# Sums of weight blocks made by accumulating DMAs instead of VectorE and GpSimd, in a float32 hybrid convolution block

## The chip, the cores and the metric

The kernel runs on one core of one Trainium2 chip. A core has TensorE (PE; its weight load is listed apart as PEld), VectorE (DVE), ScalarE (ACT), GpSimd (POOL) and SyncE (SP, which only issues DMAs), and 16 DMA engines that all queues share. The metric is the device time of one execution in microseconds; a comparison uses the median of several runs.

## What is computed

One block on a sequence of 1024 positions with 1024 channels, all in float32. Cut to what matters here:

```python
h = rms_norm(x, norm_mix_g) * (1.0 + sc1) + sh1
b_s, c_s, v_s, v_c, gl_c, gate_br = split(h @ w_in)          # 7 x 1024 columns
y_a = (b_s * causal_dwconv(c_s * v_s, conv_short_w)) @ w_short_out
u = causal_dwconv(v_c * sigmoid(gl_c), conv_conf_w) + conv_conf_b
y_b = silu(layer_norm(u, conf_ln_g, conf_ln_b)) @ w_conf_out
g_a, g_b = split(sigmoid(gate_br))
x = x + g1 * ((g_a * y_a + g_b * y_b) @ w_o)
h2 = rms_norm(x, norm_ffn_g) * (1.0 + sc2) + sh2
a, b = split(h2 @ w_ffn_in)
x = x + g2 * ((silu(a) * b) @ w_ffn_out)
return rms_norm(x, final_norm_g)
```

## The kernel before

**Products.** Two tricks shape the work. First, a float32 product is made of three passes of TensorE: an operand is split into a rounded part (`wh`, a copy on ACT, line 234) and a remainder (`wl`, a subtraction, line 235, on DVE or POOL), and likewise the activations (`th`, `tl`); then wh by th, wh by tl and wl by th are added up in PSUM (`mm3`, lines 397, 398 and 400). Second, the large products are done by Strassen's scheme in Winograd's form: a pair of output row blocks, called a *dual*, has four weight blocks of 128 x 1024 ("11", "12", "21", "22"), and seven products stand in place of eight. They run in the order `PRODUCTS = "1265734"`. Product 1 uses block 11 and product 2 block 12. Product 6 uses s2 = 11 + (21 + 22), product 5 uses s1 = 21 + 22, product 7 uses 21 + 11, product 3 uses 12 + s2 and product 4 block 22. So each dual needs four sums of weight blocks. One product is 24 matmuls of 128 x 512.

**Stages.** A lead part makes the first products of h. Then come 13 duals of the input projection (`w_duals`, the last six matrices of `w_in` and the rest of the gates; 87 products, 88 to 562 us), two duals of the short convolution's projection (`w_short`, "ya", to 643 us), the projections `w_conf` and `w_o`, and the feed-forward part, which has duals of its own (`dual_units` with DVE, `last_units`) that the change doesn't touch. Beside the 13 duals DVE computes the long convolution (`conv`, line 972) and POOL adds up its result (`tot`, line 993). In the ya stage DVE also makes the layer norm's squares (lines 1015 and 1021) and multiplies with the gates, which POOL loads from DRAM (`ga`, line 1088).

**Units.** The weights of a product are made by a *unit*: it loads blocks (SP, line 218) into `raw` tiles, makes the sums that it needs, and splits the result (`split_w`). `next_w` calls `fetch`, which keeps three units begun: the one in use and two ahead. There are five `raw` tiles in turn (three of `rawp`, two of `rawbp`), and three `wh` and three `wl` tiles. So the rounding of a unit waits until TensorE has left the `wh` of the unit three before it.

**Who sums and splits.** The 13 duals are in three groups. Dual 0 has everything on DVE. Of dual 1 the units 1, 2 and 5, and of dual 2 the units 1 and 2, are on DVE, the rest on POOL. Duals 3 to 12 are wholly on POOL, sums and remainders. Both ya duals are on DVE. Duals 0 to 2 and the ya duals use `apart_units`, which loads blocks shortly before use, some of them twice; duals 3 to 12 use `dual_units`, which loads the four blocks once, with unit 1, and sums in lines 254, 257, 259 and 301. The sums of `apart_units` are line 312.

**Order.** A planner puts each engine's instructions in an order when the kernel is built, by its own estimate of when each is ready, with the order of the program as priority; `tc.issue_after(x)` holds an instruction behind x on the same engine. On the chip each engine then takes its instructions strictly in that order, and waits where one isn't ready. A DMA that needs data of another one waits on the queue of the engine that issues it.

Of the kernel before, what the change touches and what calls it, by code (L numbers as in the profile page):

```python
# [38 lines left out]
ALU = mybir.AluOpType  # L39
# [28 lines left out]
BEGUN = 2  # L68
# [47 lines left out]
PRODUCTS = "1265734"  # L116
# [15 lines left out]
def block_kernel(ctx: ExitStack, tc: tile.TileContext, x0, xT, c, vecs, ada, w_first, w_plain, w_duals,  # L132
                 w_short, w_conf, w_o, w_fi, w_fo0, w_fo1, outT):
    nc = tc.nc
# [42 lines left out]
    def f32(t):  # L177
        return t.bitcast(F32)
# [30 lines left out]
    def raw_tile(n=1024, home=None):  # L209

        if home is None:
            raws.append(raws.pop(0))
        return (home or raws[-1]).tile([P, 1024], F32, tag="raw", name="raw")[:, :n]

    def load(src, n=1024, home=None):
        raw = raw_tile(n, home)
        with tc.issue_after(x1_load[0]) if x1_load else ExitStack():
            load.ins = nc.sync.dma_start(raw, src).ins
        return raw
# [8 lines left out]
    def split_w(raw, n, after=(), lo_engine=nc.vector):  # L228
        wh = whp.tile([P, 1024], F32R, tag="wh", name="wh")[:, :n]
        wl = wlp.tile([P, 1024], F32R, tag="wl", name="wl")[:, :n]  # L230
        with ExitStack() as order:
            for ins in after:
                order.enter_context(tc.issue_after(ins))
            hi = nc.scalar.copy(wh, raw)  # L234
            lo = lo_engine.tensor_tensor(wl, raw, f32(wh), ALU.subtract)  # L235
        split_w.hi, split_w.lo = hi.ins, lo.ins
        if n == T and lo_engine is nc.gpsimd:
            pool_los.append((hi.ins, lo.ins))
        return wh, wl

    def dual_units(mats, n, early=0, eng=nc.vector):


        a = {}

        def get(*blocks):
            for b in blocks:
                a[b] = load(mats[("11", "12", "21", "22").index(b)], n)

        def sums(which, after=None):  # L250

            if "1" in which:
                a["s1"] = a["22"] if early == 2 else raw_tile(n)
                eng.tensor_tensor(a["s1"], a["21"], a["22"], ALU.add)
            with tc.issue_after(after) if after else ExitStack():
                if "3" in which:
                    eng.tensor_tensor(a["21"], a["21"], a["11"], ALU.add)
                if "2" in which:
                    dual_units.ins = eng.tensor_tensor(a["11"], a["11"], a["s1"], ALU.add).ins

        def begin():

            with tc.issue_after(load.ins):
                get("21", "22")
            yield
            eng.tensor_tensor(a["22"], a["21"], a["22"], ALU.add)
            with tc.issue_after(load.ins):
                get("11")
            yield
            a["s2"] = s2p.tile([P, T], F32, tag="x1", name="s2")[:, :n]  # L270
            with tc.issue_after(mix.half_0):
                eng.tensor_tensor(a["s2"], a["11"], a["22"], ALU.add)
            yield

        def unit_begun(m):
            get(*{"1": ("11",), "2": ("12",), "5": ("21", "22"), "7": ("11", "12"), "4": ("22",)}.get(m, ()))
            if m == "5":
                sums("1")
            elif m == "7":
                sums("3")  # L280
                eng.tensor_tensor(a["12"], a["12"], a["s2"], ALU.add)
            return split_w(a[{"1": "11", "2": "12", "6": "s2", "5": "s1", "7": "21", "3": "12", "4": "22"}[m]], n, (), eng)

        def unit(m, after=None):
            if "s2" in a:
                return unit_begun(m)
            if early == 2:
                get(*{"1": ("11",), "2": ("12",), "6": ("21", "22", "11"), "3": ("12",), "4": ("22",)}.get(m, ()))
            elif early:
                get(*{"1": ("11",), "2": ("12", "21", "22", "11")}.get(m, ()))  # L290
            elif m == "1":
                get("11", "12", "21", "22")
            if m in "12":
                w = split_w(a["1" + m], n, (), eng)
                if eng is nc.gpsimd:
                    sums("13" if m == "1" else "2")
                return w
            if m == "6" and eng is not nc.gpsimd:
                sums("132", after)
            if m == "3":  # L300
                eng.tensor_tensor(a["12"], a["12"], a["11"], ALU.add)
            return split_w(a[{"6": "11", "5": "s1", "7": "21", "3": "12", "4": "22"}[m]], n, (), eng)

        return {m: (lambda *after, m=m: unit(m, *after)) for m in PRODUCTS} | {"begin": begin()}

    def apart_units(mats, eng, on_eng=PRODUCTS, after=None):


        a = {}

        def add(out, x, y):
            unit.eng.tensor_tensor(out, x, y, ALU.add)  # L312
            return out

        def get(b):
            return load(mats[("11", "12", "21", "22").index(b)])

        def unit(m):
            unit.eng = eng if m in on_eng else nc.gpsimd
            if m in "12":  # L320
                raw = get("1" + m)
            elif m == "6":
                for b in ("21", "22", "11"):
                    a[b] = get(b)
                with tc.issue_after(after()) if after else ExitStack():
                    a["s1"] = add(a["22"], a["21"], a["22"])
                    if "6" in on_eng:
                        raw = a["s2"] = add(raw_tile(), a["11"], a["s1"])
                    else:
                        a["s3"] = add(a["21"], a["21"], a["11"])  # L330
                        raw = a["s2"] = add(a["11"], a["11"], a["s1"])
            elif m == "7":
                raw = a["s3"] if "s3" in a else add(a["21"], a["21"], a["11"])
            elif m == "3":
                raw = get("12")
                add(raw, raw, a["s2"])
            else:
                raw = a["s1"] if m == "5" else get("22")
            return split_w(raw, 1024, (), unit.eng)

        return {m: (lambda m=m: unit(m)) for m in PRODUCTS}

    plan = [None] * KC
    plan += [(w_plain[0], 1024)]
    n_duals = len(PAIRS) // 2
    win_units = [apart_units([w_duals[d, m] for m in range(4)], nc.vector, PRODUCTS if d == 0 else "125" if d == 1 else "12",
                             (lambda: t_split.ins) if d == 1 else None) for d in range(BEGUN + 1)]
    win_units += [dual_units([w_duals[d, m] for m in range(4)], 1024, eng=nc.gpsimd) for d in range(BEGUN + 1, n_duals)]
    win_order = [(BEGUN, m) for m in "12"] + [(d, m) for d in range(BEGUN + 1) for m in PRODUCTS[2:]]
    win_order += [(d, m) for d in range(BEGUN + 1, n_duals) for m in PRODUCTS]  # L350
    plan += [win_units[d][m] for d, m in win_order]
    ya_order = [(d, m) for m in "12" for d in range(2)] + [(d, m) for d in range(2) for m in PRODUCTS[2:]]
    ya_units = [apart_units([w_short[d, m] for m in range(4)], nc.vector) for d in range(2)]
    plan += [ya_units[d][m] for d, m in ya_order]
    plan += [(w[k], 1024) for w in (w_conf, w_o) for ks in (range(KC), SECOND[KEPT:]) for k in ks]
    ready = []
# [186 lines left out]
    x = {}  # L543
# [351 lines left out]
    b = {}  # L895
# [794 lines left out]
```

## Time and profile before

| What | us |
|---|---|
| median of 3 runs (1460.18 to 1462.07) | 1462.01 |
| the profiled execution | 1462.66 |
| its span, first to last instruction | 1460.9 |
| busy: PE, DVE, ACT, POOL | 1448.1, 1188.5, 627.2, 516.3 |

The profile is a page about one execution, and a trace that can be asked for more: groups of instructions, waits, the DMA issues with their time to landing, and timelines. A row of a timeline has the start, the duration, the engine, the line of the kernel, the operation, what it writes and reads, and how often it stands there in a row; in brackets, how long the engine was idle before it and what ended that. A row on one tile has the smallest, the median and the largest duration in ns, and the first and last start in us. Matmuls are pipelined and their ends are modelled, so their starts tell more than their durations.

### The profile page before, as it was taken

Reading aid. Unit: us, or ns where it says so; the run is one execution under the profiler, and the core shown is the slowest. Engines: PE = TensorE matmul, PEld = TensorE weight load, DVE = VectorE, ACT = ScalarE, POOL = GpSimd, SP = SyncE. Lnnn points to the kernel's source line nnn. Section 1 sums busy time; section 2 is a strip of 40 time slices with the busy share of each in tenths; the row PEclk is TensorE's granted clock in tenths of the full one; section 3 lists DMA queues with packets and bytes.
Section 4 is the critical chain, followed back from the end, with each engine's and each line's share of the span. In section 5 each row is a group of like instructions: output and inputs, shape, how many; then the busy total and the mean of one; then the engine's idle time right before and its main releaser. Section 6 shows DMA issues by size and latency. Waiting matters only on the chain.

```text
span 1460.9 us, 17711 instructions
## 1 busy us (share of the span) xinstructions
PE 1448.1 (99%) x6394; PEld 1187.8 (81%) x6394; DVE 1188.5 (81%) x1634; ACT 627.2 (43%) x911; POOL 516.3 (35%) x484
## 2 busy tenths in 40 slices
PE   9999999999999999999999999999999999999997
PEld 4878888888888888788888888888888888888887
DVE  7897999987988979999787698777777666866676
ACT  4773333333333346465235465444444443322235
POOL 0007777677677761111021001111111005662505
PEclk9999999999999999999999999999999999999999
DMA  9542222323222357476685436655554449996903
GB/s 351 206 139 85 73 94 79 116 73 101 72 87 73 123 201 281 130 233 206 209 293 203 152 101 216 214 178 198 169 177 148 143 148 327 395 392 193 359 1 116
DMA packets 88522, 257.68 MB, mean 176 GB/s; under 512 B 10177, under 2 KB 12865, under 8 KB 88434
## 3 DMA queue, kind: packets, MB, share of 16 engines
q1 hardware_dynamic: 43792, 142.04, 29.1%
q0 software_dynamic: 40608, 101.92, 21.2%
q10 hardware_dynamic: 4034, 12.59, 2.4%
q8 instruction: 50, 0.82, 0.2%
q14 instruction: 38, 0.31, 0.1%
HBM read 190.97 MB, written 65.54 MB: 176 GB/s over the span
## 4 chain that ended last, share of the span: by engine, by line
PE 88%; issue 4%; DVE 3%; POOL 2%; DMA 1%; ACT 1%; POOLq 0%; DVEq 0%; ACTq 0%
PE bank L400 11%; PE bank L397 11%; PE bank L398 11%; PE x L400 8%; PE x L398 8%; PE x L397 8%; PE z L397 3%; PE z L398 3%; PE z L400 3%; PE mix L400 2%; PE mix L397 2%; PE yb L400 2%; PE yb L397 2%; PE mix L398 2%; PE yb L398 2%
## 5 line engine op out<-in xcount | busy, mean ns | idle before, releaser
L234 ACT CAST wh<-raw 128x1024 fp32r<-128x1024 f32 (+3 forms) x255 | 260.9, 1026 | 475.5 <-PE bank L398 149.5
L235 DVE TENSOR_TENSOR wl<-raw,wh 128x1024 fp32r<-128x1024 f32 (+3 forms) x176 | 209.1, 1190 | 49.3 <-ACT wh L234 46.6
L235 POOL TENSOR_TENSOR wl<-raw,wh 128x1024 fp32r<-128x1024 f32 x79 | 191.4, 2426 | 105.4 <-ACT wh L234 105.3
L972 DVE SCALAR_TENSOR_TENSOR c<-diff,vec,c 128x512 f32<-128x512 f32 x232 | 168.4, 752 | 2.7
L1331 POOL DMA_DIRECT2D hid<-stage x70 | 37.3, 533 | 343.9 <-DVE stage L438 332.5
L400 PE MATMUL bank<-th,wl 128*128 128x512 f32 x312 | 121.5, 389 | 0.4 <-POOL wl L235 0.4
L398 PE MATMUL bank<-tl,wh 128*128 128x512 f32 x312 | 121.4, 389 | 0.0
L397 PE MATMUL bank<-th,wh 128*128 128x512 f32 x312 | 121.4, 389 | 0.0
L972 DVE SCALAR_TENSOR_TENSOR c<-u,wsum,c 128x512 f32<-128x512 f32 x112 | 84.4, 753 | 2.3
L400 PEld LDWEIGHTS bank<-th,wl 128*128 128x128 f32 x312 | 58.6, 188 | 13.0 <-POOL wl L235 0.8
L398 PEld LDWEIGHTS bank<-tl,wh 128*128 128x128 f32 x312 | 58.6, 188 | 12.2
L398 PE MATMUL x<-tl,wh 128*128 128x512 f32 x176 | 68.5, 389 | 0.0
L397 PE MATMUL x<-th,wh 128*128 128x512 f32 x176 | 68.5, 389 | 0.0
L400 PE MATMUL x<-th,wl 128*128 128x512 f32 x176 | 68.4, 390 | 0.0
L397 PEld LDWEIGHTS bank<-th,wh 128*128 128x128 f32 x312 | 58.6, 188 | 12.1
L437 ACT CAST stage<-g 128x512 fp32r<-128x512 f32 x60 | 37.3, 621 | 68.0 <-DMA hid<-stage 42.9
L438 DVE TENSOR_TENSOR stage<-g,stage 128x512 fp32r<-128x512 f32 x60 | 41.3, 690 | 27.2 <-ACT stage L437 27.1
L1355 POOL DMA_DIRECT2D th<-hid x77 | 41.2, 535 | 53.5 <-PE x L400 23.4
L312 POOL TENSOR_TENSOR raw<-raw 128x1024 f32<-128x1024 f32 x8 | 20.5, 2567 | 110.0 <-ACT th L437 104.9
L400 PE MATMUL yb<-zsh,wl 128*128 128x512 f32 x128 | 49.8, 389 | 0.0
L397 PE MATMUL yb<-zsh,wh 128*128 128x512 f32 x128 | 49.8, 389 | 0.0
L398 PE MATMUL yb<-zsl,wh 128*128 128x512 f32 x128 | 49.8, 389 | 0.0
(829 smaller groups left out, 4135.4 us busy)
## 6 DMA issues: line engine op xcount, KB each, us to landing
hid<-stage POOLq DMA_DIRECT2D x70, 512.0 KB, 4.7
raw<-in_w_duals SPq DMA_DIRECT2D x57, 512.0 KB, 3.5
raw<-in_w_fi SPq DMA_DIRECT2D x54, 512.0 KB, 4.7
th<-hid POOLq DMA_DIRECT2D x77, 256.0 KB, 6.0
tl<-hid POOLq DMA_DIRECT2D x77, 256.0 KB, 6.1
ada<-in_ada SPq DMA_DIRECT2D x24, 512.0 KB, 5.7
raw<-in_ada SPq DMA_DIRECT2D x24, 512.0 KB, 4.9
raw<-in_w_fo SPq DMA_DIRECT2D x16, 512.0 KB, 6.1
```

The source lines that it names most:

```text
L234: hi = nc.scalar.copy(wh, raw)
L235: lo = lo_engine.tensor_tensor(wl, raw, f32(wh), ALU.subtract)
L312: unit.eng.tensor_tensor(out, x, y, ALU.add)
L397: nc.tensor.matmul(ps, wh, xh, start=first, stop=False, skip_group_check=again)
L398: nc.tensor.matmul(ps, wh, xl, start=False, stop=False, skip_group_check=again)
L400: mm3.ins = nc.tensor.matmul(ps, wl, xh, start=False, stop=last, skip_group_check=again).ins
L437: t_split.act = nc.scalar.copy(hi, src).ins
L438: t_split.ins = nc.vector.tensor_tensor(lo, src, f32(hi), ALU.subtract).ins
L972: tap.ins = nc.vector.scalar_tensor_tensor(out=out, in0=src[:, s : s + H], scalar=wt, in1=acc, op0=ALU.mult, op1=ALU.add).ins
L1331: nc.gpsimd.dma_start(hid_dram[key], s)
L1355: nc.gpsimd.dma_start(t, hid_dram[key][:, s])
```

## The change

`apart_units` is replaced by `sum_units`, which serves all 13 input duals and both ya duals. Each sum is an accumulating DMA that POOL issues: the first block is loaded by SP as before, and the DMA adds the second block, from DRAM, onto it in the `raw` tile. For s2 the second operand is s1, from its own `raw` tile. So s2 waits for two loads and one accumulation, and s1 stays as it is for unit 5. Product 3's weights are made in the tile of s2. Which engine makes the remainder of which unit stays the same (`on_vector`).

```diff
-    def apart_units(mats, eng, on_eng=PRODUCTS, after=None):
+    def sum_units(mats, on_vector=PRODUCTS):
...
             if m in "12":
-                raw = get("1" + m)
+                raw = load(mat["1" + m])
             elif m == "6":
-                for b in ("21", "22", "11"):
-                    a[b] = get(b)
-                with tc.issue_after(after()) if after else ExitStack():
-                    a["s1"] = add(a["22"], a["21"], a["22"])
-                    if "6" in on_eng:
-                        raw = a["s2"] = add(raw_tile(), a["11"], a["s1"])
-                    else:
-                        a["s3"] = add(a["21"], a["21"], a["11"])
-                        raw = a["s2"] = add(a["11"], a["11"], a["s1"])
+                a["s1"] = load(mat["22"])
+                nc.gpsimd.dma_start(a["s1"], mat["21"], accum_op=ALU.add)
+                raw = a["s2"] = load(mat["11"])
+                nc.gpsimd.dma_start(raw, a["s1"], accum_op=ALU.add)
             elif m == "7":
-                raw = a["s3"] if "s3" in a else add(a["21"], a["21"], a["11"])
+                raw = load(mat["21"])
+                nc.gpsimd.dma_start(raw, mat["11"], accum_op=ALU.add)
             elif m == "3":
-                raw = get("12")
-                add(raw, raw, a["s2"])
+                raw = a["s2"]
+                nc.gpsimd.dma_start(raw, mat["12"], accum_op=ALU.add)
             else:
-                raw = a["s1"] if m == "5" else get("22")
-            return split_w(raw, 1024, (), unit.eng)
+                raw = a["s1"] if m == "5" else load(mat["22"])
+            return split_w(raw, 1024, (), nc.vector if m in on_vector else nc.gpsimd)
...
-    win_units = [apart_units([w_duals[d, m] for m in range(4)], nc.vector, PRODUCTS if d == 0 else "125" if d == 1 else "12",
-                             (lambda: t_split.ins) if d == 1 else None) for d in range(BEGUN + 1)]
-    win_units += [dual_units([w_duals[d, m] for m in range(4)], 1024, eng=nc.gpsimd) for d in range(BEGUN + 1, n_duals)]
+    win_units = [sum_units([w_duals[d, m] for m in range(4)], (PRODUCTS, "125", "12", "")[min(d, BEGUN + 1)])
+                 for d in range(n_duals)]
...
-    ya_units = [apart_units([w_short[d, m] for m in range(4)], nc.vector) for d in range(2)]
+    ya_units = [sum_units([w_short[d, m] for m in range(4)]) for d in range(2)]
```

More of the change, by code (lines that the diff above doesn't have):

```diff
@@ L304, in dual_units @@
         return {m: (lambda *after, m=m: unit(m, *after)) for m in PRODUCTS} | {"begin": begin()}
-    def apart_units(mats, eng, on_eng=PRODUCTS, after=None):
+    def sum_units(mats, on_vector=PRODUCTS):
         a = {}
[L311 to L316, printed above, removed]
+        mat = dict(zip(("11", "12", "21", "22"), mats))
         def unit(m):
-            unit.eng = eng if m in on_eng else nc.gpsimd
             if m in "12":
-                raw = get("1" + m)
+                raw = load(mat["1" + m])
             elif m == "6":
-                for b in ("21", "22", "11"):
-                    a[b] = get(b)
-                with tc.issue_after(after()) if after else ExitStack():
-                    a["s1"] = add(a["22"], a["21"], a["22"])
-                    if "6" in on_eng:
-                        raw = a["s2"] = add(raw_tile(), a["11"], a["s1"])
-                    else:
-                        a["s3"] = add(a["21"], a["21"], a["11"])
-                        raw = a["s2"] = add(a["11"], a["11"], a["s1"])
+                a["s1"] = load(mat["22"])
+                nc.gpsimd.dma_start(a["s1"], mat["21"], accum_op=ALU.add)
+                raw = a["s2"] = load(mat["11"])
+                nc.gpsimd.dma_start(raw, a["s1"], accum_op=ALU.add)
             elif m == "7":
-                raw = a["s3"] if "s3" in a else add(a["21"], a["21"], a["11"])
+                raw = load(mat["21"])
+                nc.gpsimd.dma_start(raw, mat["11"], accum_op=ALU.add)
             elif m == "3":
-                raw = get("12")
-                add(raw, raw, a["s2"])
-            else:
-                raw = a["s1"] if m == "5" else get("22")
-            return split_w(raw, 1024, (), unit.eng)
+                raw = a["s2"]
+                nc.gpsimd.dma_start(raw, mat["12"], accum_op=ALU.add)
+            else:
+                raw = a["s1"] if m == "5" else load(mat["22"])
+            return split_w(raw, 1024, (), nc.vector if m in on_vector else nc.gpsimd)
         return {m: (lambda m=m: unit(m)) for m in PRODUCTS}
```

## The prediction

> **What bounds the kernel now.** I read the page's first part, then PE's waits (who waited for whom: us in total, times, longest), then busy time by stretch (the stretch, its length, then PE, PEld, DVE, ACT and POOL with their counts, clock, DMA share, GB/s), and last the timelines of the two places where PE waits.
>
> ```profile
> PE 1448.1 (99%) x6394; PEld 1187.8 (81%) x6394; DVE 1188.5 (81%) x1634; ACT 627.2 (43%) x911; POOL 516.3 (35%) x484
> ...
> PE bank L400 <- DVE wl L235: 0.5, 1, 0.5
> PE bank L400 <- POOL wl L235: 0.4, 1, 0.4
> PE lead L398 <- DVE h41l L488: 0.3, 1, 0.3
> PE z L397 <- DVE g L1296: 0.2, 1, 0.2
> ...
> 156.00:535.00 379.00, 379.00 (x1674) 313.83 (x1673) 337.14 (x487) 135.03 (x184) 282.10 (x124) 1.00 0.27 89
> 535.00:645.00 110.00, 109.45 (x474) 88.61 (x473) 103.65 (x135) 62.90 (x96) 22.09 (x25) 1.00 0.68 230
> ```
>
> PE is busy for 99% of the span. A modelled end can hide a gap, so I look at the starts as well.
>
> ```profile
> 246.66 0.39 PE L397 MATMUL bank<-h41h,wh 128*128 128x512 f32 x1
> ...
> 252.10 0.39 PE L397 MATMUL bank<-th,wh 128*128 128x512 f32 x1
> ...
> 257.54 0.39 PE L397 MATMUL bank<-h00h,wh 128*128 128x512 f32 x1
> ...
> 268.42 0.39 PE L397 MATMUL bank<-t2h,wh 128*128 128x512 f32 x1
> ...
> 148.24 0.39 PE L398 MATMUL bank<-tl,wh 128*128 128x512 f32 x1
> 149.05 0.50 PE L400 MATMUL bank<-th,wl 128*128 128x512 f32 x1 [0.42 <-POOL wl L235]
> ...
> 612.68 0.39 PE L400 MATMUL bank<-q4h,wl 128*128 128x512 f32 x1
> 613.09 0.50 PE L397 MATMUL bank<-q6h,wh 128*128 128x512 f32 x1
> 613.43 0.39 PE L398 MATMUL bank<-q6l,wh 128*128 128x512 f32 x1
> 614.35 0.50 PE L400 MATMUL bank<-q6h,wl 128*128 128x512 f32 x1 [0.53 <-DVE wl L235]
> 614.69 0.40 PE L397 MATMUL bank<-q6h,wh 128*128 128x512 f32 x1
> ```
>
> The first four rows are the first matmuls of the products 3 and 4 of one dual and of 1 and 6 of the next. From 246.66 to 252.10 are 5.44 us for 24 matmuls, 0.227 us each, and 257.54 to 268.42 is twice that: PE runs at its own pace. From 156 to 535 us it never waits. Only two waits of PE lie where the changed sums are made. At 148 us a matmul starts 0.81 us after the one before it, 0.58 over the pace, and the one behind it 0.11 late: 0.7 us, for a remainder on POOL. At 613 us the four steps of 0.41, 0.34, 0.92 and 0.34 are 1.1 us over four times 0.227, for a remainder on DVE. Together 1.8 us: that is all that the change can give here, 0.12% of the time. (A measurement of this kernel tells about 0.2%, 2.9 us, from no change.)
>
> **What is removed.**
>
> ```profile
> L312 DVE TENSOR_TENSOR raw<-raw x12: 1220/1224/1240, 77.8 to 623.7; 128x1024 f32<-128x1024 f32 x12
> ...
> L312 POOL TENSOR_TENSOR raw<-raw x8: 2395/2400/3269, 107.8 to 144.2; 128x1024 f32<-128x1024 f32 x8
> ...
> L254 POOL TENSOR_TENSOR raw<-raw x10: 2402/2407/2412, 169.4 to 511.4; 128x1024 f32<-128x1024 f32 x10
> ...
> 144.24 2.40 POOL L312 TENSOR_TENSOR raw<-raw 128x1024 f32<-128x1024 f32 x1 [1.30 <-DMA raw<-in_w_duals]
> 146.59 7.12 POOL L235 TENSOR_TENSOR wl<-raw,wh 128x1024 fp32r<-128x1024 f32 x3
> ...
> 597.71 1.22 DVE L312 TENSOR_TENSOR raw<-raw 128x1024 f32<-128x1024 f32 x1
> ...
> 608.33 1.23 DVE L312 TENSOR_TENSOR raw<-raw 128x1024 f32<-128x1024 f32 x1
> ...
> 610.67 1.23 DVE L312 TENSOR_TENSOR raw<-raw 128x1024 f32<-128x1024 f32 x1
> ...
> 613.07 1.23 DVE L235 TENSOR_TENSOR wl<-raw,wh 128x1024 fp32r<-128x1024 f32 x1
> ```
>
> Sixty sums, four for each of 15 duals. DVE loses 12 of 1.22 us, 14.7 us, of which 8 lie in the short projection's stage. POOL loses 8 of 2.4 us (L312) and four for each of the ten duals that it sums itself (L254 and its like L257, L259, L301): 48 in all, 115 us. Neither engine bounds anything from 156 to 535 us, where POOL is busy 282 of 379 us and PE never waits, so there the gain is nothing. It is 0.7 us at 148 us, where POOL held the late remainder (146.59) behind a sum that had stood for a DMA (144.24). It is 1.1 us at 613 us, where DVE ran without a pause and took two sums (608.33, 610.67) right ahead of the remainder that PE waited for (613.07): without them that one is 2.4 us earlier, with the sum at 597.71 gone too 3.7, more than it was late.
>
> **What is added: 60 accumulating DMAs of 512 KB, issued by POOL, and 15 loads more on SP.** An input dual that POOL summed takes four loads now, and six loads and four accumulations afterwards. From 156 to 535 us the DMA engines are busy 0.27, so two and a half times as many transfers stay under 0.7; from 535 to 645 us the share is 0.68, and there 14 loads become 12 with 8 accumulations on top, which press on it for a while. Such an accumulation isn't in this trace. The nearest rows:
>
> ```profile
> raw<-in_w_duals SPq DMA_DIRECT2D x57, 512.0 KB, 3.5
> ...
> hid<-stage POOLq DMA_DIRECT2D x70, 512.0 KB, 4.7
> ...
> x<-x_dram POOLq DMA_DIRECT2D x8, 512.0 KB, 5.6
> ...
> cv<-cv SPq DMA_DIRECT2D x8, 512.0 KB, 7.0
> ...
> ga<-gate_a POOLq DMA_DIRECT2D x16, 256.0 KB, 4.1
> ...
> L1331 POOL DMA_DIRECT2D hid<-stage x70 | 37.3, 533 | 343.9 <-DVE stage L438 332.5 <-ACT stage L437 7.8 <-issue 2.9
> ```
>
> Issuing costs POOL 0.53 us, 32 us for sixty, against the 115 us taken off. The landing time L lies between 3.5 us (a load by SP of the same size) and 11.2 us (twice the 5.6 us of a DRAM-to-SBUF load by POOL, since the destination is read as well); I take 5.6, the same direction, size and queue. What L costs depends on what waits for it. POOL has to wait for the first accumulation of unit 6 (21 onto 22) before it issues the second (that sum onto 11), and behind it wait its next remainders. In the steady part, one dual to the next:
>
> ```profile
> 237.31 2.40 POOL L235 TENSOR_TENSOR wl<-raw,wh 128x1024 fp32r<-128x1024 f32 x1
> ...
> 242.37 2.40 POOL L235 TENSOR_TENSOR wl<-raw,wh 128x1024 fp32r<-128x1024 f32 x1 [2.66 <-ACT wh L234]
> ...
> 246.68 1.05 ACT L234 CAST wh<-raw 128x1024 fp32r<-128x1024 f32 x1 [3.90 <-issue]
> ```
>
> A rounding on ACT starts when PE leaves the wh buffer three units back: that of the next dual's unit 1 at 246.68, with product 3. Its remainder could end at 250.2 and is wanted at 257.54, so there are some 7 us to lose. After the change, block 22 of the next dual takes the buffer of the sum s2, free when the remainder of unit 3 ends (237.31 + 2.40 = 239.7), and has landed by 243.2. The first accumulation goes out behind the remainder of unit 4 at 244.8, the second at 244.8 + L, and it lands at 244.8 + 2L. Two things must hold. The remainder of unit 1, queued behind the second issue, ends at 244.8 + L + 0.5 + 2.4 and is wanted at 257.54: L up to 9.8. Unit 6 has rounding and remainder to come, 3.5 us, and is wanted at 268.42: 244.8 + 2L + 3.5, so L up to 10.1. With 5.6 us both keep over 4 us, and the price is nothing; with 11.2 us unit 6 is 2.3 us late in each of ten duals. The accumulations of units 7 and 3 stand alone and have at least as much time. ACT has evacuation copies queued behind the rounding of unit 6; at L = 5.6 the sum lands at 256.0, before PE frees wh at 257.54, so that ACT waits no longer than it does.
>
> On this the Trainium skill has a rule that speaks against the change: "Collectives: The Full Stack", in the section on the bandwidth ceiling, says that a DMA that adds reads two sources and so moves its bytes at half the rate of a copy. No run here shows it yet. As a mechanism of this kernel: 256 KB by POOL land in 4.1 us and 512 KB in 5.6, so the data part of 512 KB is 3.0 us, and doubled it makes L = 8.6 us (an estimate from these two rows). That is still under 9.8, and the sum stays as it is, with 1.2 us left instead of 4.
>
> In the first duals (91 to 156 us) POOL makes no sum before 107.8 us (the first start in the row of L312), so the accumulations of dual 0 go out as their blocks land. In the short projection the remainders stay on DVE, which waits for nothing new unless a sum is late. The one that mattered, for unit 6 of its second dual, can be ready long ahead: the buffer of its last block falls free at 587.95 (SP's row under the second rival), load 3.5, accumulation 5.6, so 597 against 612. The new wait there is for POOL's queue, which holds the loads of the gates (second rival).
>
> The raw buffers turn over five; before, 84 draws are made up to the end of this stage, after it 86, so that later stages find the ring turned by two. I price that at nothing, since after 645 us the list of PE's waits has only 0.2 us (for g, L1296); it can go either way by about that.
>
> **Sum.** The profiled execution took 1462.66 us, 1460.9 of it span. Less 0.7 and 1.1, plus nothing: 1460.9 us. The median of the runs shown, 1462.01, is 0.65 us below the profiled one; from it the same sum gives 1460.2.
>
> **Rivals.**
>
> *Accumulations land late (slower).* Place: unit 6 of each dual; it decides from L = 9.8 us. At 11.2 us it costs 10 times 2.3 us: 1484 us. For it: two reads for each byte, and cv<-cv shows 7.0 us for a plain load among traffic. Against it: DMA share 0.27. A worse form is an order by program: were the first accumulation queued behind the remainder of unit 2 (about 255.6), unit 6 would need 255.6 + 2L + 3.5 under 268.42, L under 4.7, and 5.6 us would cost 1.9 us a dual, 1480 us. Against that form: the planner now puts unit 3's sum (L301) ahead of the remainders of 6, 5 and 7. Together 0.26.
>
> *The gates' loads stand behind an accumulation (slower).*
>
> ```profile
> 587.95 0.33 SPq L218 DMA_DIRECT2D raw<-in_w_short  x1
> ...
> 588.82 1.13 POOL L1088 DMA_DIRECT2D ga<-gate_a  x2 [8.42 <-DVE ma L747]
> ...
> 593.55 1.31 DVE L747 TENSOR_TENSOR ma<-y,ga 128x512 f32<-128x512 f32 x2 [0.22 <-DMA ga<-gate_a]
> 595.37 1.22 DVE L235 TENSOR_TENSOR wl<-raw,wh 128x1024 fp32r<-128x1024 f32 x1
> ```
>
> DVE already waits 0.22 us for a gate, and the remainder at 595.37 ends at 596.6, just as product 7 starts. If POOL stands 3.5 us for a block ahead of that load, DVE and then PE lose up to that, once (1464.4, still within 0.2%) or twice (1468: it decides from the second time). Against it: DVE has 10 us less to do in this stage. 0.13.
>
> *The relief is eaten by a new order (no change).* The 0.7 us came from a sum that stood for a DMA ahead of a remainder on POOL, and there will be more such DMAs: 1462.7. It lies within 0.2% like the forecast; I give it 0.17 and the forecast 0.40.
>
> *More is gained.* Beyond the two waits, PE's list has 0.3 us for h41l and 0.2 us for g besides its clock matmuls of the first microseconds; only with all of these, and steps that they delay, would it be 1459 us or below: 0.04.
>
> **Chances.** Forecast and no-change case: within 0.2% 0.57. Slower 0.39. Faster 0.04. The range goes from 1459.3 (a little under the sum from the median) up to 1484, the first rival's price; beyond both ends lies about 0.16. The likeliest case alone: 1459.5 to 1463.
>
> **What would show it.** Right: landing near 5.6 us in the DMA issues, PE's waits at 148 and 613 us gone, no new wait of PE on wl or wh, POOL's busy time some 85 us lower (115 off, 32 on) and DVE's 14.7 lower. Wrong: PE waiting for wh or wl once in every dual (first rival; the step from product 2 to 6 longer than 5.44 us), DVE idle before L747 on a gate's load (second). The forecast falls if L passes 9.8 us or if the planner puts a waiting accumulation ahead of a remainder that has no time to lose.

## The result, and the profile after

The kernel after takes 1468.59 us (median of 6 runs, 1466.69 to 1470.0), the kernel before in the same comparison 1461.95 us (6 runs, 1460.18 to 1462.2). The ratio is 1.0048, 95% interval 1.0037 to 1.0059: slower by 6.6 us, where 1460.9 us, no change that a measurement can tell, was forecast. The profiled execution of after took 1468.51 us, 1466.7 of it span; its mean granted clock is 0.996, where the one of before has 0.999.

The page's first row, then PE's waits (total us, times, longest):

```profile
PE 1450.6 (99%) x6394; PEld 1189.8 (81%) x6394; DVE 1168.4 (80%) x1622; ACT 626.1 (43%) x911; POOL 453.2 (31%) x496
...
PE bank L385 <- DVE ma L735: 4.3, 1, 4.3
...
PE y L385 <- ACT y L1085: 0.4, 1, 0.4
```

POOL lost 63 us and DVE 20, and still there is one new wait of 4.3 us: for `ma`, the product of a bank of the short convolution's projection (the ya stage) with a gate. Busy time by stretch:

```profile
156.00:535.00 379.00, 379.00 (x1672) 313.54 (x1671) 333.27 (x485) 135.47 (x185) 220.44 (x124) 1.00 0.68 172
535.00:645.00 110.00, 105.27 (x444) 84.93 (x444) 90.96 (x122) 60.60 (x94) 27.35 (x29) 0.97 0.79 246
```

From 156 to 535 us, where two thirds of the sums lie, PE is as busy as before; the two and a half times as many transfers (DMA share 0.68 for 0.27) are hidden. What is lost lies between 535 and 645 us, and there the granted clock is 0.97. The issues with their landing times:

```profile
raw<-in_w_duals SPq DMA_DIRECT2D x74, 512.0 KB, 3.7
...
raw<-in_w_duals POOLq DMA_DIRECT2D x39, 512.0 KB, 5.7
...
raw<-raw POOLq DMA_DIRECT2D x15, 512.0 KB, 5.3
raw<-in_w_short SPq DMA_DIRECT2D x12, 512.0 KB, 6.1
...
cv<-cv SPq DMA_DIRECT2D x8, 512.0 KB, 9.2
...
raw<-in_w_short POOLq DMA_DIRECT2D x6, 512.0 KB, 6.7
```

The POOLq rows are the accumulations: medians of 5.7 us (thirteen duals), 5.3 (thirteen of its fifteen in these duals) and 6.7 (ya). Medians hide the crowd: the three accumulations that go out in ya between 565 and 580 us need 10.5, 10.9 and 8.6 us. In ya the plain loads beside them became slower too: `cv<-cv` 9.2 us for 7.0, the weight blocks by SP 6.1 for 3.9.

How the 4.3 us arise is read from the chain of work that ended last (start, duration, what):

```profile
574.04 13.33 DMA raw<-in_w_short
...
588.19 6.60 DMA ga<-gate_a
```

and from the timelines of POOL, DVE and PE at that place:

```profile
587.65 0.86 POOL L317 DMA_DIRECT2D raw<-in_w_short  x1 [8.10 <-DMA raw<-in_w_short]
588.19 1.45 POOL L1076 DMA_DIRECT2D ga<-gate_a  x2
...
594.88 1.29 DVE L735 TENSOR_TENSOR ma<-bank,ga 128x512 f32<-128x512 f32 x2 [7.52 <-DMA ga<-gate_a]
...
591.01 0.39 PE L388 MATMUL bank<-q6h,wl 128*128 128x512 f32 x1
595.72 0.76 PE L385 MATMUL bank<-q5h,wh 128*128 128x512 f32 x1 [4.32 <-DVE ma L735]
596.28 0.63 PE L386 MATMUL bank<-q5l,wh 128*128 128x512 f32 x1
596.71 0.63 PE L388 MATMUL bank<-q5h,wl 128*128 128x512 f32 x1
```

A weight block of the second ya dual was loaded at 574.04 us and needed 13.33 us to land. POOL stood 8.10 us for it, to add a second block to it (L317). The first two loads of the gates (L1076) were next on POOL's queue and went out at 588.19 us and right behind, where the kernel before sends them at 578.13 and 579.86. They landed 6.6 us later, DVE stood idle 7.52 us for them, `ma` could start at 594.88, and PE, whose bank `ma` reads, went on at 595.72. From 591.01 to 595.72 is 4.5 us over the pace of 0.227. And then the matmuls start 0.43 us apart instead of 0.227, 13 of them. The clock column (the one before the DMA share) says why:

```profile
594.00:598.00 4.00, 2.28 (x6) 1.82 (x7) 3.12 (x6) 0.54 (x2) 2.02 (x3) 0.55 0.38 134
598.00:602.00 4.00, 4.00 (x12) 3.19 (x11) 4.00 (x7) 3.63 (x7) 0.00 (x0) 0.59 0.88 208
```

The granted clock fell to one half for 6.8 us, of which PE worked 5.5: 13 steps, 0.2 too long each, are another 2.7 us. So this place costs 7.2 us. The account by starts of the matmuls, before against after: 7.2 at this place; 1.0 at 90 us, for the remainder of dual 0's unit 6 (its second accumulation goes out only at 82.42 us, the row of POOL below); 0.6 at 580 us, where ACT's copies stand behind the rounding of a sum that landed 10.5 us after its issue; 0.1 net in single places; less 0.7 at 148 us, 1.1 at 613 us and 0.5 at 914 us, and less 1.1 in the first microseconds, which differ between executions of one kernel: 5.5, against 5.8 between the spans.

```profile
82.42 0.88 POOL L319 DMA_DIRECT2D raw<-raw  x1 [8.46 <-DVE t2l L426]
```

### The profile page after: what moved, and what is told of

Same layout as the page of the kernel before. It is cut to its first block, busy times and chain, and to the rows that moved or that the text cites. A ratio compares the mean times of both kernels' runs of the same rounds, so it can differ in the third digit from the quotient of the medians.

```text
span 1466.7 us, 17801 instructions
## 1 busy us (share of the span) xinstructions
PE 1450.6 (99%) x6394; PEld 1189.8 (81%) x6394; DVE 1168.4 (80%) x1622; ACT 626.1 (43%) x911; POOL 453.2 (31%) x496
## 4 chain that ended last, share of the span: by engine, by line
PE 92%; DMA 2%; DVE 2%; POOL 1%; issue 1%; ACT 0%; POOLq 0%; DVEq 0%; ACTq 0%
PE bank L388 12%; PE bank L385 12%; PE bank L386 12%; PE x L388 8%; PE x L386 8%; PE x L385 8%; PE z L388 4%; PE z L386 4%; PE z L385 4%; PE y L386 2%; PE y L385 2%; PE y L388 2%; PE mix L388 2%; PE yb L386 2%; PE yb L388 2%; PE mix L386 2%
## 5 line engine op out<-in xcount | busy, mean ns | idle before, releaser
L235 POOL TENSOR_TENSOR wl<-raw,wh 128x1024 fp32r<-128x1024 f32 x79 | 199.6, 2585 | 71.8 <-ACT wh L234 71.8
L254 DVE TENSOR_TENSOR raw<-raw 128x1024 f32<-128x1024 f32 (+1 forms) x15 | 17.8, 1188 | 43.7 <-DMA raw<-in_w_fi 30.4
```

## The experiments

**Which sums cost it.** My theory was the ya stage alone; the rival, a little in every dual. First only ya by accumulating DMA, then all but ya. Edits, against before and against after:

```diff
-    ya_units = [apart_units([w_short[d, m] for m in range(4)], nc.vector) for d in range(2)]
+    ya_units = [sum_units([w_short[d, m] for m in range(4)]) for d in range(2)]
```

> The kernel before with the short projection's sums alone made by accumulating DMAs. Queue theory: GpSimd's order in this stage is that of the changed kernel, so the whole loss is here: a stall of 4 to 5 us on the gates plus 2 to 3 us of low clock, 1467 to 1469 us. Input duals as the cause: no loss, 1461 to 1463.

Measured: 1470.13 us (5 runs), ratio 1.0064, interval 1.0052 to 1.0076.

```profile
PE bank L423 <- DVE ma L773: 4.2, 1, 4.2
PE z L423 <- DVE g L1322: 2.4, 1, 2.4
```

The eight accumulations of ya alone (four sums in each of two duals) bring the same wait for `ma`, with its half clock 6.0 us by the starts. A second wait, for `g` in the feed-forward part at 914 to 921 us, was 0.2 us in before and is 2.4 here; it makes the loss larger than that of after.

```diff
-    ya_units = [sum_units([w_short[d, m] for m in range(4)]) for d in range(2)]
+    ya_units = [apart_units([w_short[d, m] for m in range(4)], nc.vector) for d in range(2)]
```

> The changed kernel with the short projection's eight sums back on VectorE (the 13 input duals keep their accumulating DMAs). Queue theory (the loss is GpSimd's queue: the first accumulation of the second short dual waits there for its block, ahead of the gates' loads): the stall of 4.5 us near 591 us and the low clock behind it are gone, the wait of 1.1 us at 613 us of the kernel before is back; 1461 to 1463 us. Traffic theory (the accumulations' extra bytes make the gates and blocks late): the same here, since the stage's traffic is as before. If it were the input duals that lose the time, it would stay at 1467 to 1470.

Measured: 1465.63 us (6 runs), ratio 1.0032, interval 1.0019 to 1.0044. A miss: the wait for `ma` is gone, but the time isn't back.

```profile
PE z L422 <- DVE g L1321: 3.1, 1, 3.1
```

The wait for `g` came up here too, at a place where no sum is changed; with its half clock it is 6.0 us in the profiled execution, at 1470.11 us the slowest of the six. It is settled below. A cleaner cut leaves the accumulations of ya out of the kernel after (the expectation says ten, they are eight). By the two traces DVE, ACT, PE and SP have the same order in that stage as in after:

```diff
-                nc.gpsimd.dma_start(a["s1"], mat["21"], accum_op=ALU.add)
+                if add:
+                    nc.gpsimd.dma_start(a["s1"], mat["21"], accum_op=ALU.add)
...
-    ya_units = [sum_units([w_short[d, m] for m in range(4)]) for d in range(2)]
+    ya_units = [sum_units([w_short[d, m] for m in range(4)], add=False) for d in range(2)]
```

> The kernel after with the ten accumulations of the short convolution's projection left out and everything else as it is: those weight blocks are then plain blocks and not sums, so this part of the computation is not the reference's. Theory, the loss in this stage is that of the accumulations themselves, in the queue and in the transfers: no wait of PE over 1 us between 585 and 620 us, the ring's phase stays that of the kernel after, and the time is that of the change in the thirteen duals alone, 1460 to 1462.5. Rival, it comes from VectorE's and ScalarE's order, which the change moved, or from the blocks' loads, which were put later: the wait at 591 us stays, 1465 to 1469.

Measured: 1460.97 us (11 runs), ratio 1.0000, interval 0.9991 to 1.0009.

```profile
535.00:645.00 110.00, 110.00 (x479) 89.72 (x478) 97.61 (x131) 64.80 (x98) 22.42 (x25) 1.00 0.66 226
```

PE never waits in that stage, and the clock is 1.00. So the loss of 0.48% comes from the eight accumulations themselves, not from a new order of the engines, and the other 52 neither gain nor cost anything that can be measured.

**The queue or the late landing.** Is it only that the gates' loads stand behind an accumulation on POOL's queue? Then putting them ahead should cure it (`GATES_FIRST` is 4 in the first of two runs and 2 in the second):

```diff
+                with tc.issue_after(gates[-1]) if gates else ExitStack():
+                    nc.gpsimd.dma_start(a["s1"], mat["21"], accum_op=ALU.add)
...
+            if len(gates) < GATES_FIRST:
+                gates.append(first)
```

> The changed kernel with one order changed: the first accumulation of the second short dual is queued behind the first four loads of the gates instead of ahead of them; the same sums, the same transfers. Queue theory: VectorE's wait of 7.5 us for the gate falls below 2 us, no stall of TensorE over 1 us near 591 us, no low clock; 1460.5 to 1462.5 us. Traffic theory: the gates land as late as before, stall of 3 us or more, 1466 to 1469 us.

Measured: 1462.9 us (12 runs, 1461.04 to 1467.38), ratio 1.0014, interval 1.0006 to 1.0022: a little above the queue theory's range, far below the rival's. The wait for `ma` is gone, and one of 1.9 us has come at 614 us. Its chain:

```profile
PE bank L391 <- DVE wl L236: 2.3, 2, 1.9
...
602.91 10.08 DMA ga<-gate_a
613.09 0.58 DVE ma L742
...
615.60 1.15 DVE wl L236
```

Here the fifth and sixth gate are late. They go out right behind another accumulation, at 602.91 us, and need 10.08 us to land; DVE is idle 6.54 us for them, and the remainder that PE wants is queued behind. The next expectation puts this wait down to late accumulations of the weight block; the trace doesn't bear that out, for ACT rounds that block's sum at 606.42 us, well ahead of its product.

> The kernel after, with the first accumulation of the short convolution's dual 1 held behind the first two of the gates' loads in place of the first four. With four, the 4.3 us wait at 591 us went and one of 2.3 us came at 614 us, because the accumulations of that block were then late. Theory, the wait at 591 us is only that of the first two loads, which stand behind the accumulation on GpSimd's queue: with two the accumulation waits for its block anyway (landed at 587), the first gates come some 8 us earlier, and neither wait is there: 1460.8 to 1462.2. Rival, the third and fourth gate are late by as much as the first were: a wait of 2 to 4 us at 597 to 605 us, with the halved clock, 1464 to 1469.

Measured: 1465.41 us (10 runs, 1462.93 to 1466.55), ratio 1.0028, interval 1.0019 to 1.0038. A miss: the time is in the rival's range, and the third and fourth gate are late, as it said, but not because they go out late.

```profile
577.90 1.43 POOL L1079 DMA_DIRECT2D ga<-gate_a  x2
...
587.91 1.13 POOL L1079 DMA_DIRECT2D ga<-gate_a  x2
...
595.00 1.31 DVE L738 TENSOR_TENSOR ma<-y,ga 128x512 f32<-128x512 f32 x2 [2.58 <-DMA ga<-gate_a]
...
PE bank L391 <- DVE wl L236: 1.5, 1, 1.5
```

All four go out as early as in before (578.13, 579.86 and twice from 588.82 us on), but the first two need 8.9 to 9.0 us to land, for 3.1 to 4.1 there, and the next two 7.0 for 4.6. DVE is idle 2.58 us for the latter, and a remainder queued behind is late for PE, by 1.5 us and without a fall of the clock; this execution, at 1462.93 us, is the fastest of the ten. None of the three orders on the one queue is free of a wait. So the gates got a queue of their own, and the same move was made in before:

```diff
-            nc.gpsimd.dma_start(ga, gate_dram["a", j][:, halves[h]])
+            nc.scalar.dma_start(ga, gate_dram["a", j][:, halves[h]])
```

> The kernel after with the sixteen gates' loads of the short convolution issued from ScalarE's queue in place of GpSimd's; the accumulations stay where they are. Theory, the loss is that of one in-order queue: a gate's load stands behind an accumulation that waits for its block (first two loads at 588.2 and 588.7 us where the kernel before has 578.1 and 579.9), and where it is put ahead the accumulation is late instead. With two queues neither waits for the other: no wait of PE over 1 us between 585 and 620 us, 1460 to 1462.5. Rival, the accumulations' traffic makes the blocks and gates land late whatever queue they stand in (the block before 587 took 13.3 us in place of 3.5): a wait of 2 us or more stays between 585 and 620 us, 1463.5 to 1468.5. A third, ScalarE's own queue is held up by a gate's load that waits for its buffer: waits for ScalarE's hi or copies, over 1463.5 too.

> The kernel before with the same sixteen loads on ScalarE's queue: what the move costs or gains by itself. Before, nothing stands ahead of these loads on GpSimd's queue, so both theories expect no gain: 1460 to 1462.5; over 1463.5 the move itself holds ScalarE up, and the run with the accumulations is then to be read against this one.

Measured: after with that move 1463.57 us (8 runs), ratio 1.0019, interval 1.0009 to 1.0029; before with it 1461.67 us (11 runs), ratio 1.0005, interval 0.9996 to 1.0014, so the move itself is free. In the first, PE's wait and the chain into it:

```profile
PE bank L388 <- DVE wl L235: 1.6, 2, 1.4
...
566.48 10.46 DMA raw<-raw
...
577.01 1.05 ACT wh L234
...
582.37 6.78 DMA ga<-gate_a
...
592.93 1.15 DVE wl L235
```

The gates go out 6 us earlier than in after, and the wait for `ma` is gone. A wait of 1.4 us for a remainder stays, between my theory's 1 us and the rival's 2; the time is at the lower edge of the rival's range. Both have a share: of the 0.48%, 0.29% went with the queue and 0.19% stayed, each with some 0.1% of uncertainty. What stays begins with a late landing, as the chain above shows: an accumulation takes 10.46 us, ACT rounds its sum at 577.01, and the gates, behind that on ACT, go out at 582.37 (at 578.97 in before with the same move) and need 6.78 us. Issues and landing times from 565 to 590 us, first this kernel, then the one with the accumulations left out:

```profile
raw<-in_w_short SPq DMA_DIRECT2D x3, 512.0 KB, 14.0
...
ga<-gate_a ACTq DMA_DIRECT2D x3, 256.0 KB, 6.8
```

```profile
raw<-in_w_short SPq DMA_DIRECT2D x4, 512.0 KB, 5.2
...
ga<-gate_a POOLq DMA_DIRECT2D x4, 256.0 KB, 4.6
```

With accumulations in flight the one block whose landing the trace has needs 14.0 us, and a gate 6.8 in the median; without them it is 5.2 (two blocks) and 4.6. In before with the gates on ACT's queue it is 2.9 for a gate. So the gates' own queue doesn't spare them the late landing.

**The wait at 914 us.** The draws from the five raw buffers up to the end of ya were 84 in before, 86 in after, 90 and 80 in the two kernels above. If the phase of the ring sets that wait, it must come by turning the ring in before, where nothing else is changed, and go by turning it in the kernel with ya on VectorE:

```diff
+    first, n_conf = len(plan) - len(SECOND[KEPT:]) * 2 - 2 * KC, plan[-len(SECOND[KEPT:]) * 2 - 2 * KC]
+    plan[first] = lambda: (raws.extend(raws[:TURN]), raws.__delitem__(slice(TURN)), weights(*n_conf))[-1]
```

> The kernel before, nothing added or taken away but the order of the five raw buffers: after the short convolution's last weight block the list of pools is turned by one, so that the next block takes the buffer that it would have taken one draw later. In the four kernels run so far the wait of PE for VectorE's g at 914 to 919 us was 0.3 to 0.6 us where the draws up to there were 84 (before), none at 86 (after, and after with the gates first), 3.1 us at 90, 2.4 at 80 and 2.1 at 92: by the remainder of five 4, 1, 0, 0 and 2. Theory, the ring's phase sets that wait: here the phase is 0, so the wait is 2 to 3 us, with the halved clock behind it in some of the runs: 1463.5 to 1467. Rival, the wait comes from where the accumulations put the transfers or from the order of the whole program, and the phase has no part in it: within 0.15% of before, 1459.5 to 1463.7, and the wait stays below 0.7 us.

> The kernel after with the short convolution's sums on VectorE again, and the ring of raw buffers turned by one behind its last block, which brings the phase from 0 to 1, that of the kernel after. Theory, the ring's phase: the 3.1 us wait for g at 919 us and its halved clock (5.7 us together in the untimed part of the trace) go, and what is left is the change in the thirteen duals alone: 1461 to 1462.5. Rival, the phase has no part in it: the wait stays and the time is that of the kernel without the turn, 1464 to 1470.

Measured: before, turned, 1464.85 us (8 runs), ratio 1.0023, interval 1.0013 to 1.0033; the kernel with ya on VectorE, turned, 1461.7 us (11 runs), ratio 1.0005, interval 0.9996 to 1.0014, and no wait there. Both as the theory had it. How the phase acts is seen in the issues from 904 to 910 us, first of before turned, with its wait, then of before:

```profile
raw<-in_w_fi SPq DMA_DIRECT2D x2, 512.0 KB, 4.3
hid<-stage POOLq DMA_DIRECT2D x2, 512.0 KB, 5.9
...
PE z L400 <- DVE g L1299: 2.9, 1, 2.9
```

```profile
hid<-stage POOLq DMA_DIRECT2D x2, 512.0 KB, 3.1
```

With the ring turned, two weight blocks find their buffers free just here and are loaded beside two stores of the hidden layer, which take 5.9 us instead of 3.1. The three `stage` buffers come free later, ACT and then DVE wait for one, and the evacuation `g` is queued behind DVE's. In after the ring happens to stand well: the 0.5 us that the profiled execution of before loses here are gone. That is no merit of the accumulations, and other executions at before's phase lose 0.3 us here or nothing.

**The price of a wait.** Does the halved clock belong to the wait or to the accumulations? Eight operations that change nothing make DVE late in before:

```diff
             ma[j, h] = s_tile(f"ma{j}{h}")
+            for _ in range(STALL if len(ma) == 1 else 0):
+                nc.vector.tensor_tensor(ga, ga, ga, ALU.max)
             op(ma[j, h], ps, ga)
```

> The kernel before with eight operations on VectorE that change nothing (a maximum of a gate's tile with itself, 128x512, 0.6 us each) ahead of the first product of the gates in the short convolution; other operations come between them by VectorE's order, so that this product starts some 10 us later, at about 595 us, as in the kernel after. There is no accumulation in it. Theory, PE's wait of about 4 us alone halves the granted clock behind it, for 3.4 or 6.8 us, and so costs 1.5 to 3 us more than its length: a wait of 3 to 5.5 us at 591 us, and 1466 to 1469. Rival, the halved clock of the kernel after belongs to the accumulations' traffic: the same wait with the clock at 1.0 behind it, 1464 to 1466.5.

Measured: 1470.83 us (4 runs), ratio 1.0073, interval 1.006 to 1.0087. PE's wait, and the clock behind it:

```profile
PE bank L398 <- DVE ma L748: 7.9, 1, 7.9
...
594.00:598.00 4.00, 0.00 (x0) 0.00 (x0) 4.00 (x6) 1.56 (x2) 0.00 (x0) 0.66 0.45 136
598.00:602.00 4.00, 3.35 (x8) 2.71 (x9) 4.00 (x7) 3.46 (x7) 0.00 (x0) 0.50 0.02 7
```

The wait is longer than I expected, and so is the time. The clock is halved behind it with no accumulation in the kernel: the price belongs to the wait. An earlier attempt put the same operations under a condition (`len(ma) == 2`) that never holds, because the dictionary also keeps an entry of another kind; its instructions are those of before:

> The kernel before with eight operations on VectorE that change nothing (a maximum of a tile with itself, 128x512) ahead of the second product of the gates in the short convolution, where the kernel after was late: VectorE is late by eight times 0.6 us, 4.8 us, once, and nothing else is changed. Theory, a wait of PE of 2 us or more halves its granted clock for 3.4 to 6.8 us and so costs 1.5 to 3 us more than its length: a wait of 3 to 4.8 us, then 7 to 15 products steps of 0.43 in place of 0.227 us, span 1464.5 to 1468.5. Rival, the halved clock in the kernel after comes from the accumulations (their traffic, or the loads in flight): the same wait with the clock at full behind it, span 1463.5 to 1465.7.

Measured: 1460.88 us (1 run), span 1459.1. It tells nothing of the clock. As a repeat of before it tells one thing: the 1.1 us wait at 613 us isn't there.

**Dual 0.** Last, its sums back on VectorE in the kernel that has those of ya there already:

```diff
+    win_units = [apart_units([w_duals[0, m] for m in range(4)], nc.vector)]
+    win_units += [sum_units([w_duals[d, m] for m in range(4)], (PRODUCTS, "125", "12", "")[min(d, BEGUN + 1)])
+                  for d in range(1, n_duals)]
```

> As the first run, with the sums of input dual 0 on VectorE too, where the changed kernel shows a step of 0.9 us at 90 us because the second accumulation of unit 6 lands at 88.6 us. If that step comes from the accumulations' landing of 6 to 9 us there, it is gone: 0.5 to 1 us less than the first run. If not, the same time as the first run.

Measured: 1471.55 us (5 runs), ratio 1.0065, interval 1.0052 to 1.0078. A miss, and it doesn't tell what dual 0 costs:

```profile
PE bank L424 <- DVE tl L464: 3.2, 1, 3.2
PE z L423 <- DVE g L1322: 2.1, 1, 2.1
```

The step at 90 us is gone in this trace, as the theory had it, but two other waits have come. The chain into the first:

```profile
108.59 9.25 DMA raw<-in_w_duals
...
118.12 4.57 DMA raw<-raw
...
124.87 1.95 DVE tl L464
```

VectorE's sums stand among its splits of the activations at 98 to 102 us, the load that waits for their buffer goes out at 103.74, and behind it come the two accumulations of dual 1, of which the first needs 9.25 us. The second wait, for `g`, belongs to the ring, which stood at another phase again. So the price of dual 0 can't be read from this time. In the other kernels with its accumulations the step at 90 us is 0.5 to 1.0 us, or missing (two gates first; ya's sums left out).

## Why the prediction was wrong

**The step that failed** is the one on the short projection: "DVE, which waits for nothing new unless a sum is late", with the new wait named and left at nothing, and given 0.13 as the second rival. That rival's mechanism and place were right: POOL stands for a block ahead of the gates' loads. Its size was not. It was worked out with 3.5 us for a block to land, taken from a stage without accumulations; among them it took 13.3 us, and so the stand was 8.1 us and the gates 10 us late. The prediction said that the eight accumulations would "press on it for a while" and gave that no number: the gates that came late took 6.6 to 10.1 us to land, where before has 3.1 to 4.7 for the same ones, and an accumulation took up to 10.9 us, where L was 5.6. That is the part which stayed when the gates went out in time. And "DVE has 10 us less to do in this stage" was no argument against it: DVE stood idle 7.5 us for a gate. The measured time lies inside the stated range and near the rival's 1468 for two waits, both by luck: the range reaches so far for the first rival, which didn't come, and there was one wait, with a half clock behind it that the prediction had not priced.

**The price of a wait** was counted as its length. The halved clock behind it made 7.2 us of 4.5. The run with eight idle operations shows this without any accumulation. The Trainium skill ("TensorE: Matmul & The Clock Gate", section "Why this matters for your kernels") asks for no idle gaps of PE over about 3 us, because the clock then falls to half. The measured 0.43 us for 0.227 agree with a half; but here the clock also fell behind a single wait of 1.9 us (four gates first), and there the measurement decides:

```profile
616.00:620.00 4.00, 3.21 (x9) 2.60 (x10) 4.00 (x7) 1.26 (x2) 0.90 (x1) 0.69 0.56 123
```

**Landing and steady part: right.** L was taken as 5.6 us and measured at 5.3 to 5.7 in the duals, and PE's time from 156 to 535 us is unchanged in the profiled execution; other kernels with the same duals show one wait there, for a remainder on POOL at 295 us, of up to 0.8 us over the pace. By the rule of the Trainium skill's "Collectives: The Full Stack" (section on the bandwidth ceiling) the estimate was 8.6; the duals' medians don't bear out a doubled data part. The first rival, at 0.26, didn't come.

**The two gains.** 0.7 us at 148 us came: the wait is in all six traces whose duals keep their sums on the engines and in none of the eight with accumulations. The 1.1 us at 613 us came in the profiled execution, but the term was read from one execution: the repeat of before, before turned and before with its gates on ACT don't have that wait.

**Engine time and the ring.** Issuing was put at 0.53 us by a store's row, and POOL's relief at 83 us:

```profile
L235 POOL TENSOR_TENSOR wl<-raw,wh 128x1024 fp32r<-128x1024 f32 x79 | 199.6, 2585 | 71.8 <-ACT wh L234 71.8
...
160.91 0.88 POOL L317 DMA_DIRECT2D raw<-in_w_duals  x1 [4.07 <-DMA raw<-in_w_duals]
161.51 2.70 POOL L235 TENSOR_TENSOR wl<-raw,wh 128x1024 fp32r<-128x1024 f32 x1
```

An accumulation occupies POOL for 0.88 us, so the sixty cost 53 us and not 32; the sums that went took 117 us by before's rows, and 64 is the difference, 63 what POOL's busy time lost. The remainders' mean of 2585 ns, 2426 before, looks like another cost and is none: behind an issue a remainder is recorded as begun while the issue still runs, and it ends 2.42 us after the issue's end (161.79 to 164.21), no later than one that stands alone. DVE lost 20 us where 14.7 were forecast; the rest lies in operations that the change leaves as they are, and why they took less isn't settled. None of this reaches PE. The ring's turn was priced at nothing with ±0.2 us by the list of PE's waits. It gave 0.5 us here, and the same term is 2.9 us of wait at the wrong phase: the list shows what a phase costs, not what another one would. Dual 0, priced at nothing, shows 1.0 us.

## What to carry to other kernels

Work that is taken off an engine and put on a DMA queue waits there in order: look at what stands behind it on that queue, and compute that with landing times of the stage as it will be, loads beside accumulations, not as it was. An engine's relief is worth only the waits that end on it, here 1.8 us for 63 us of POOL's time. Where PE is never idle, a wait of about 2 us and more can bring a half clock behind it, which costs 1.5 to 3 us more; here it did so in seven cases and not in two.

## What the runs showed of the hardware

- Behind waits of PE the granted clock stood at one half: 4.5 us over the pace cost 7.2 here. Every fall inside a run lasts 3.41 us, or 6.83 where the wait went on past the fall, and every change of the clock lies a whole number of 3.41 us after the first one of its execution (in after, 172 of them). In these traces a fall goes with the way a wait lies on this grid. By the matmuls' starts the clock fell where PE had stood 2.0 us (four gates first), 2.2 (dual 0, at 925 us), 3.2 (after) or more of the 3.41 ahead of the fall. It stayed up where the grid cut the wait in two, 1.8 and 1.3 us (before, turned) or 1.6 and 1.0 us (ya alone, at 921 us). In these traces the limit lies near 2 us; one part of 2.05 us passed without a fall.
- An accumulating DMA of 512 KB lands in 5.3 to 5.7 us in the median, against 3.7 for a load by SP, and occupies POOL for 0.88 us.
- Where accumulations and plain loads crowd each other (DMA share 0.95 from 565 to 590 us of after), a load of 512 KB took up to 14 us and an accumulation up to 10.9 us.
- An instruction of POOL behind an accumulation's issue can be recorded as begun 0.3 us before the issue ends, so that the mean of its durations grows (2585 ns for 2426) though its end comes no later.
